# Two MLP norms moved earlier and pinned, a projection's weight split taken off GpSimd, and two roots moved, in a two-block fp32 model on one Trainium2 core

## Chip, cores and metric

The kernel runs on 1 core of one Trainium2 chip (trn2). The metric is device time in microseconds, the median of three runs. The program has 16154 instructions on five engines: TensorE (PE), VectorE (DVE), ScalarE (ACT), GpSimd (POOL) and SyncE (SP), which issues nearly all DMAs.

## What is computed

A sequence of 256 tokens with 1024 channels goes through two layers, then through a third block with other attention; all in float32. The parts that the change touches:

```python
def rmsnorm(x, g):
    y = xf * lax.rsqrt(jnp.mean(xf * xf, axis=-1, keepdims=True) + EPS)
    return (y * g.astype(jnp.float32)).astype(x.dtype)

def mixer_c(h, ...):                       # layer 1
    gate, xr = jnp.split(h @ w_in, 2, axis=-1)
    xr = causal_depthwise_conv(xr, conv_w) + conv_b
    y = rg_lru(xr, w_r, b_r, w_i, b_i, lam) * jax.nn.gelu(gate)
    return y @ w_out

def first_block(x, ...):
    for layer in range(DEPTH):             # DEPTH = 2
        h = rmsnorm(x, mix_norm[layer])
        y = mixer_ab(h, ...) if layer % 2 == 0 else mixer_c(h, ...)
        x = x + y
        x = x + sq_relu_mlp(rmsnorm(x, mlp_norm[layer]), w_up[layer], w_down[layer])
    return rmsnorm(x, final_norm)
```

`sq_relu_mlp` is `square(relu(h @ w_up)) @ w_down` with 4096 hidden channels. The second block ends with a projection, a gated residual and one more RMS norm.

## The kernel before

Activations lie with channels on the 128 partitions and the 256 tokens along the free axis. All weights, 242 units of 128 x 1024 floats (512 KB), are read from HBM once, in the order of their use. `fetch` puts a unit into one of 4 `raw` buffers by a DMA on SP's queue; `prep` (L321 to L326) splits it into a rounded part `wh` (a copy, on ACT at L323 or on DVE at L325) and the rest `wl = raw - wh` (L326, on DVE or POOL). The table `POLICY` (from L43) says which engine does which part of which unit: "ag" is ACT and POOL, "av" ACT and DVE, "vv" DVE twice. Split units stand in rings named `wh`/`wl` and `wxh`/`wxl`.

Each product is three matmuls of 128 x 256, high by high (L383), low by high (L384) and high by low (L385); a unit used for a product of 8 x 128 rows is 24 matmuls. `gpair` makes a block pair of 512 columns from two units; `krow` adds one row block `k` of a projection into four accumulators.

`mlp` (from L967) runs `p` from 0 to 15. Step `p` makes a pair of hidden blocks, `up(p)`: 48 matmuls on PE, a ReLU on ACT (`mr`, L987), the rounded square on ACT (`mah`, L988), the exact square on POOL (`ma`, L989), their difference on DVE (`mal`, L435). From `p` = 2 on it adds rows `k` = 2p-4 and 2p-3 of the down projection: 24 matmuls each. The norm of `x` is not applied to the inputs of `up` but at the end, as a factor 1/(mean square + eps), since the squared ReLU is homogeneous. That factor needs: squares on ACT and their sums on POOL (`ssq`, L437), a sum over channels on PE (`csum`, 128 x 1 matmuls, L452), mean and eps on DVE (`meaneps`, L458), a reciprocal on DVE (L1009), and `spread` (L473): `across` on PE puts the value on all partitions (128 x 128 matmuls with the identity, L470), ACT copies it (`R2`, L476). R2 is used by the projection's last rows, far behind. Layer 0's MLP also works off a list of background steps on DVE (`mod_setup`, `softplus`: rows `mdump` L915 and `sm`), one at each unit.

`layer1` (from L1027) is written in the order that PE and ACT keep (`inorder`). Its end is the projection `wo1` (`wrow(0)` to `wrow(4)`, then a tail): `root` makes the recurrence (L1106 and the scans L1108), `done(p)` multiplies with the gate (L1119) and splits the result for PE (`xr` by ACT, `ysl` by DVE L435); `more(n)` fetches and splits `n` more units.

Except where such pins stand, a scheduler in the compiler sets the order on each engine from dependencies and its own estimates, and the engines then run that order strictly, each waiting on semaphores.

`b2_kv`, `b2_attn` and `b2_out` make the second block. `b2_out` has the spread of the residual's scale (`R1`, the root of the first block's final norm) at its step p = 1, and at the end the last norm: column sums `stat` on PE (L1580), mean and eps on DVE (L458), the power -0.5 on POOL (`rsq`, L463), `across` on PE, and the multiplications of `xo` on DVE (L1614) ahead of the output DMAs.

Of the kernel before, what the change touches and what calls it, by code (L numbers as in the profile page):

```python
# [11 lines left out]
F32 = mybir.dt.float32  # L12
F32R = mybir.dt.float32r
AF = mybir.ActivationFunctionType
ALU = mybir.AluOpType
# [3 lines left out]
D = 1024  # L19
NK = 8  # L20
FF = 4096
EPS = 1e-6
# [21 lines left out]
POLICY = {n: ("ag",) for n in ("gate", "val", "q", "k", "v", "wo0")}  # L44
POLICY.update(val=("av", "ag", "av", "ag"), gate=("av", "av", "av", "ag"), xr=("av",), ri=("av",), cg=("av", "av", "av", "av", "ag", "ag", "ag", "ag"))
POLICY["wo0"] = ("ag",) * 7 + ("av",)
POLICY["up"] = ("ag",) * 4 + ("av",) * 60
POLICY["wo1"] = ("ag",) * 4 + ("av",) * 4
PADC = 30

COLS = {}
# [198 lines left out]
class Kern:  # L250
# [181 lines left out]
        self.nc.vector.scalar_tensor_tensor(l, xs, g, h.bitcast(F32), op0=ALU.mult, op1=ALU.subtract)  # L432

    def lo(self, l, src, h):
        self.nc.vector.tensor_tensor(l, src, h.bitcast(F32), op=ALU.subtract)  # L435

    def ssq(self, pool, x3):  # L437
        nc = self.nc
# [111 lines left out]
    def layer0(self, lp):  # L550
# [271 lines left out]
        for j in range(4):  # L822
            V.tensor_tensor(conv[:, j], conv[:, j], M, op=ALU.subtract)
        R2 = self.across(r2)
        yp(8, self.lasts)
# [22 lines left out]

    def proj_tail(self, acc, name, ins, gname, g0, xs, R2=None, mp=None, sums=(), after=None):

# [120 lines left out]
    def mlp(self, mp, l):  # L971
        nc = self.nc
        V, S, G, PE = nc.vector, nc.scalar, nc.gpsimd, nc.tensor
        x, xs = self.x, self.xs
        acc = [self.ps("acc") for _ in range(4)]
        A = {}
        R2 = None

        first = self.gfirst("up", xs)

        def up(p):
            ps = first[p] if p < 2 else self.gpair(("up", "up"), xs)
            r = self.t(mp, [128, 512], "mr", bufs=2)
            a = self.t(mp, [128, 512], "ma", bufs=2)
            ah = self.t(mp, [128, 512], "mah", F32R, bufs=4)
            al = self.t(mp, [128, 512], "mal", F32R, bufs=4)
            S.activation(r, ps, AF.Relu)  # L987
            S.activation(ah, r, AF.Square)  # L988
            G.tensor_tensor(a, r, r, op=ALU.mult)  # L989
            self.lo(al, a, ah)  # L990
            A[2 * p] = (ah[:, :T], al[:, :T])
            A[2 * p + 1] = (ah[:, T:], al[:, T:])

        for p in range(16):
            if l == 0 and p >= 9:
                if p == 9:
                    self.pad(self.cp, 96)
                    self.hs = [self.t(self.cp, [128, 2112], f"hc{c}", F32R) for c in "hl"]
                    self.pad(self.cp, 160)
                self.ahead = min(2 * p - 14, 13)  # L1000
            if l == 1 and p == 4:
                self.wx, self.slot = None, 0
            up(p)
            if p == 4:
                parts = self.ssq(mp, x)
            if p == 6:
                v = self.meaneps(self.csum(parts), D)
                rv = self.t(self.cp, [128, 2], "rv")
                V.reciprocal(rv, v)  # L1009
            if p == 8:  # L1010
                R2 = self.spread(mp, rv, "R2")
            if p >= 2:
                for k in (2 * p - 4, 2 * p - 3):
                    self.krow(acc, self.unit("down"), A.pop(k), k == 0, False)
        for k in range(28, 32 - NT):
            self.krow(acc, self.unit("down"), A.pop(k), False, False)
        last = l == 1
        xs = None if last else self.new_h()
        sums = [(self.s1, None), (self.s2, "fin")] if last else [(self.s1, None)]
        self.proj_tail(acc, "down", [A[k] for k in range(32 - NT, 32)], "mix", 8, xs, R2, mp, sums)  # L1020
        self.xs = xs

    def layer1(self, lp):
        nc = self.nc
        V, S, G, PE = nc.vector, nc.scalar, nc.gpsimd, nc.tensor
        x, xs = self.x, self.xs
# [9 lines left out]
        parts = [self.s1[:, 0], self.s1[:, 1]]  # L1036
# [80 lines left out]
        def done(p):  # L1117
            hp = slice(2 * p, 2 * p + 2)
            V.tensor_tensor(th[:, hp], th[:, hp], gl[:, hp], op=ALU.mult)  # L1119
            self.split(th[:, hp], ys[0][:, hp], ys[1][:, hp])  # L1120
# [4 lines left out]
        with self.inorder(*PIN):  # L1125
            conv(0, pss[0])
            conv(1, pss[1])
            self.more(3)
            self.hs, self.slot = None, self.slot % (RING + EXTRA)
            p2 = self.gpair(("xr", "xr"), xs)  # L1130
            heads(0)
            heads(1)
            gates(0, ri(0))
            conv(2, p2)
            tanhs(0)
            p3 = self.gpair(("xr", "xr"), xs)
            conv(3, p3)
            decay(0)
            decay(1)
            self.more(1)  # L1140
            cg(0)
            heads(2)
            heads(3)
            gates(1, ri(1))
            self.more(1)
            root(0)
            cg(1)
            ys = (self.t(lp, [128, 8, T], "xr", F32R), ysl)
            gelu(0)
            gelu(1)  # L1150
            done(0)
            self.more(1)
            tanhs(1)
            cg(2)
            done(1)
            decay(2)
            decay(3)
            self.more(1)
            cg(3)
            root(1)  # L1160
            gelu(2)
            gelu(3)
            self.more(2)
            acc = [self.ps("acc") for _ in range(4)]
            for k in range(4):
                if k == 2:
                    done(2)
                if k == 3:
                    done(3)
                wrow(k)  # L1170
                self.more(1 if k == 0 else 2)
            wrow(4)
        self.ahead = 2
        xs = self.new_h()
# [90 lines left out]
    def b2_kv(self, bp, ep, d):  # L1265
        nc = self.nc
        V, S, G, PE = nc.vector, nc.scalar, nc.gpsimd, nc.tensor
# [40 lines left out]
        for i in range(4):  # L1308
            w = self.unit("vb")
            for tt in range(4):  # L1310
                src = (xs, hc)[tt // 2]
                for kk in range(2):
                    k = 2 * i + kk
# [16 lines left out]
        for tt in range(4):  # L1330
            ps = self.ps()
# [5 lines left out]
        def zpair(nm, p, pool, between=None):  # L1337
            zpost(nm, p, pool, self.gp2([self.unit(nm), self.unit(nm)], xs, between))
# [8 lines left out]
        ps = self.gpair(("cq", "cq"), xs)  # L1347
# [9 lines left out]
        def cqn():  # L1357
            RQ = self.across(rq)
            for k in range(2):
                V.scalar_tensor_tensor(cf[:, k], cf[:, k], self.p("gcq", k), RQ, op0=ALU.mult, op1=ALU.mult)  # L1360
                self.split(cf[:, k], cq[0][:, k], cq[1][:, k])
        zpair("za", 1, ep, cqn)
        d.update(kb=kb, vb=vb, krh=krh, krl=krl, ck=ck, wk=wk, va=va, bp=bp)
        q8 = self.t(self.cp, [128, 2112], "hch")[:, :2048].rearrange("p (a b) -> p a b", a=8)
        for i in range(2):
            w = self.unit("uq")
            for j in range(2):
                ps = self.ps()
# [5 lines left out]
    def b2_attn(self, bp, ap, d):  # L1374
        nc = self.nc
        V, S, G, PE = nc.vector, nc.scalar, nc.gpsimd, nc.tensor
# [90 lines left out]
        tg = d["tg"] = {}  # L1467
# [24 lines left out]
        def gdone(nm, p):  # L1492
            def f(ps):
                tg[nm, p] = self.t(bp, [128, 512], f"t{nm}", bufs=2)
                S.activation(tg[nm, p], ps, AF.Tanh, scale=0.5)
            return f

        def gpair(nm, p):
# [23 lines left out]
        for i in range(n + 3):  # L1522
            if i < n:
                tag, h, qt = steps[i]
# [17 lines left out]
    def b2_out(self, op, d):  # L1542
        nc = self.nc
        V, S, G, PE = nc.vector, nc.scalar, nc.gpsimd, nc.tensor
        xs, tg = d["xs"], d["tg"]
        x = self.t(op, [128, 8, T], "xo")
# [5 lines left out]
        def yrow(k):  # L1552
            return ys[0][:, k], ys[1][:, k]
        for p in range(4):
            if p > 1:
                d["gpair"]("ga", p)
                d["gpair"]("gb", p)
                d["oproj"]("oa", p)
            d["oproj"]("ob", p)
            y = tg["ga", p]  # L1560
            V.tensor_tensor(y, y, tg["gb", p], op=ALU.add)
            self.split(self.pair(y), ys[0][:, 2 * p:2 * p + 2], ys[1][:, 2 * p:2 * p + 2])
            if p == 1:
                R1 = self.spread(op, d["r1"], "R1")
                for k in range(8):
                    V.scalar_tensor_tensor(x[:, k], x[:, k], self.p("fin", k), R1, op0=ALU.mult, op1=ALU.mult)
        def orow(w, k, ms, end):
            for m in ms:
                o = last[:, :T] if m == 7 else acc[m // 2][:, (m % 2) * T:(m % 2 + 1) * T]
                c = slice(m * 128, m * 128 + 128)  # L1570
                self.mm3(o, (w[0][:, c], w[1][:, c]), yrow(k), k == 0 and (m % 2 == 0 or m == 7), end)
        for k in range(6):
            orow(self.unit("wo2"), k, range(8), False)
        ws = [self.unit("wo2") for _ in range(2)]
        st = self.ps()
# [5 lines left out]
                          stop=end, skip_group_check=True)  # L1581
        def scale(b):
            for k in (2 * b, 2 * b + 1):
                S.activation(x[:, k], x[:, k], AF.Copy, scale=self.p("fg2", k))

        def fold(b):
            (G if b < 2 else V).tensor_tensor(sq[b][:, 0], sq[b][:, 0], sq[b][:, 1], op=ALU.add)
# [13 lines left out]
        with self.tc.issue_after(xi.ins):  # L1601
            fold(2)
        with self.tc.issue_after(si.ins):
            for b in range(1, 4):
                scale(b)
        stat(sq[0][:, 0], True)
        stat(sq[1][:, 0])
        stat(sq[3][:, 0])
        stat(sq[2][:, 0])
        stat(sq[3][:, 1], end=True)  # L1610
        RF = self.across(self.rsq(self.meaneps(st[:, :2], D)))
        for i, (k0, k1) in enumerate(((0, 1), (1, 3), (3, 5), (5, 7), (7, 8))):
            xb = x[:, k0:k1]
            V.tensor_tensor(xb, xb, self.b2(RF, k1 - k0), op=ALU.mult)  # L1614
# [22 lines left out]
```

## Time and profile before

| | us |
|---|---|
| median of 3 runs | 822.05 |
| lowest and highest run | 821.96, 824.75 |
| the profiled execution | 821.14 |
| its span | 819.4 |
| PE busy in the span | 787.9 (96%) |
| DVE, ACT, POOL busy | 576.4, 473.2, 199.0 |
| granted PE clock, mean | 0.991 |

The profiled execution is 0.91 us under the median of the runs. The span is what the trace covers; 1.7 us of the execution lie around it. A row of a timeline gives the start, the duration, the engine, the source line and the operation, and in brackets how long the engine had been idle before and what ended it. Matmuls overlap: one lasts 0.28 us by its record, and the next starts about 0.115 us after it, so the distance of starts is the price of one more matmul.

### The profile page before, as it was taken

The page shows a single profiled execution, that of the slowest core. Times are in us where ns is not written, and L with a number is a line of the kernel's source. Part 1 is how long each engine was busy: PE and PEld are TensorE (multiplying, and loading weights), DVE is VectorE, ACT ScalarE, POOL GpSimd, SP SyncE. Part 2 cuts the span into 40 slices and gives each one's busy share as a digit, 9 for nine tenths or more (in the row PEclk, how much of TensorE's full clock was granted, in tenths as well). Part 3 has the DMA queues.
Part 4 walks back from the last instruction along what each step waited for, and adds up shares of the span by engine and source line. Part 5 has one row for each costly group of instructions (what it writes and reads, how often), then busy time and mean ns, then how long its engine had stood idle before and what let it go on. Part 6 is the DMA issues. An engine that isn't in the chain of part 4 may idle for free.

```text
span 819.4 us, 16154 instructions
## 1 busy us (share of the span) xinstructions
PE 787.9 (96%) x6480; PEld 756.0 (92%) x6480; DVE 576.4 (70%) x952; ACT 473.2 (58%) x739; POOL 199.0 (24%) x151
## 2 busy tenths in 40 slices
PE   6999989999999999979999999999999999999996
PEld 5997889999999999978999999999989988889996
DVE  6999669999989787578746545557634877565843
ACT  5568656455545657877745444445626587765533
POOL 4796643011101202330531110111000022320001
PEclk9999999999999999999999999999999999999997
DMA  7874357787988832238726656664335533555531
GB/s 239 292 222 130 103 181 247 292 311 272 322 307 283 286 113 88 62 124 302 239 99 210 193 189 190 197 196 164 94 119 151 159 105 102 176 163 176 185 101 52
DMA packets 41259, 152.32 MB, mean 186 GB/s; under 512 B 4576, under 2 KB 5088, under 8 KB 39008
## 3 DMA queue, kind: packets, MB, share of 16 engines
q1 hardware_dynamic: 40752, 149.19, 55.5%
q10 hardware_dynamic: 432, 2.10, 0.7%
q8 instruction: 51, 0.84, 0.4%
q14 instruction: 24, 0.20, 0.1%
HBM read 149.17 MB, written 2.10 MB: 185 GB/s over the span
## 4 chain that ended last, share of the span: by engine, by line
PE 59%; issue 19%; DVE 8%; ACT 8%; POOL 4%; DMA 2%; SPq 0%; POOLq 0%; DVEq 0%; ACTq 0%
PE mm L383 10%; PE mm L384 10%; PE mm L385 10%; PE acc L384 7%; PE acc L383 7%; PE acc L385 7%; POOL ma L989 3%; PE acc L1423 2%; PE acc L1451 2%; PE mm L1460 2%; ACT wh L323 1%; DMA raw<-in_wst 1%; DVE wl L326 1%; PE mm L470 1%; DMA x<-in_xT 1%
## 5 line engine op out<-in xcount | busy, mean ns | idle before, releaser
L323 ACT ACTIVATE wh<-raw 128x1024 fp32r<-128x1024 f32 (+1 forms) x190 | 198.3, 1048 | 162.5 <-PE mm L384 64.2
L326 DVE TENSOR_TENSOR wl<-raw,wh 128x1024 fp32r<-128x1024 f32 (+1 forms) x159 | 197.6, 1250 | 100.1 <-ACT wh L323 98.3
L383 PE MATMUL mm<-xsh,wh 128*128 128x256 f32 x752 | 210.4, 280 | 0.0
L384 PE MATMUL mm<-xsl,wh 128*128 128x256 f32 x752 | 209.1, 278 | 0.0
L385 PE MATMUL mm<-xsh,wl 128*128 128x256 f32 x752 | 209.1, 278 | 0.0
L383 PEld LDWEIGHTS mm<-xsh,wh 128*128 128x128 f32 x752 | 141.7, 188 | 3.7 <-issue 3.3
L384 PEld LDWEIGHTS mm<-xsl,wh 128*128 128x128 f32 x752 | 141.7, 188 | 0.6 <-DVE xsl L878 0.2
L385 PEld LDWEIGHTS mm<-xsh,wl 128*128 128x128 f32 x752 | 141.3, 188 | 0.0
L989 POOL TENSOR_TENSOR ma<-mr 128x512 f32<-128x512 f32 x32 | 49.5, 1548 | 246.2 <-ACT mr L987 246.2
L384 PE MATMUL acc<-mal,wh 128*128 128x256 f32 x360 | 100.1, 278 | 1.0 <-DVE mal L435 1.0
L383 PE MATMUL acc<-mah,wh 128*128 128x256 f32 x360 | 100.3, 279 | 0.0
L385 PE MATMUL acc<-mah,wl 128*128 128x256 f32 x360 | 100.0, 278 | 0.0
L326 POOL TENSOR_TENSOR wl<-raw,wh 128x1024 fp32r<-128x1024 f32 x31 | 74.2, 2414 | 43.8 <-ACT wh L323 43.8
L323 ACT ACTIVATE wxh<-raw 128x1024 fp32r<-128x1024 f32 x47 | 49.2, 1055 | 38.8 <-DMA raw<-in_wst 34.9
L384 PEld LDWEIGHTS acc<-mal,wh 128*128 128x128 f32 x360 | 67.9, 189 | 1.2 <-DVE mal L435 1.2
L383 PEld LDWEIGHTS acc<-mah,wh 128*128 128x128 f32 x360 | 67.7, 188 | 0.0
L385 PEld LDWEIGHTS acc<-mah,wl 128*128 128x128 f32 x360 | 67.6, 188 | 0.0
L326 DVE TENSOR_TENSOR wxl<-raw,wxh 128x1024 fp32r<-128x1024 f32 x44 | 56.6, 1299 | 8.0 <-ACT wxh L323 8.0
L384 PE MATMUL mm<-xsl,wxh 128*128 128x256 f32 x208 | 58.1, 279 | 0.6 <-DVE xsl L878 0.6
L383 PE MATMUL mm<-xsh,wxh 128*128 128x256 f32 x208 | 58.3, 280 | 0.0
L385 PE MATMUL mm<-xsh,wxl 128*128 128x256 f32 x208 | 58.0, 279 | 0.0
L915 DVE CUSTOM_DVE_ANT_0 mdump<-mw,cv 128x1024 f32<-128x1024 f32 x40 | 48.7, 1217 | 2.7 <-DMA mw<-in_modw 2.6
(386 smaller groups left out, 1855.9 us busy)
## 6 DMA issues: line engine op xcount, KB each, us to landing
raw<-in_wst SPq DMA_DIRECT2D x240, 512.0 KB, 4.1
mw<-in_modw SPq DMA_DIRECT2D x12, 1024.0 KB, 7.2
nb<-in_nab SPq DMA_DIRECT2D x16, 256.0 KB, 3.7
ab<-in_alibi ACTq DMA_DIRECT2D x1, 1536.0 KB, 8.9
x<-in_xT SPq DMA_DIRECT2D x4, 256.0 KB, 4.9
cv<-in_cvec SPq DMA_DIRECT2D x1, 1024.0 KB, 4.7
cx<-in_cT SPq DMA_DIRECT2D x1, 1024.0 KB, 7.3
xd<-x SPq DMA_DIRECT2D x1, 1024.0 KB, 4.6
```

Of the source, the lines that this page charges most:

```text
L323: nc.scalar.activation(wh, r, AF.Copy)
L326: (nc.vector if lo == "v" else nc.gpsimd).tensor_tensor(wl, r, wh.bitcast(F32), op=ALU.subtract)
L383: mm(out, w[0], x[0], start=start, stop=False, skip_group_check=True)
L384: mm(out, w[0], x[1], start=False, stop=False, skip_group_check=True)
L385: return mm(out, w[1], x[0], start=False, stop=stop, skip_group_check=True)
L470: self.lasts = self.nc.tensor.matmul(ps[:, j * 128:(j + 1) * 128], rc[:, j:j + 1].to_broadcast([128, 128]), self.ident, start=True, stop=True)
L915: V.tensor_tensor_reduce(d, w, cv[:, s * 1024:(s + 1) * 1024], 0.5, 0.0, op0=ALU.mult, op1=ALU.add, accum_out=self.mod[:, s * 24 + i:s * 2 ...
L989: G.tensor_tensor(a, r, r, op=ALU.mult)
L1423: PE.matmul(sc[i], Q[tag, h][a][:, qs], K[tag, h][b], start=a + b == 0, stop=a == 1)
L1451: PE.transpose(pt[:, i * 128:(i + 1) * 128], P[:, i * 128:(i + 1) * 128], self.ident)
L1460: PE.matmul(o[64 * hh:64 * hh + 64, :T], vt[:, i, h * 64:h * 64 + 64], PTs[tag, h][:, i], start=i == 0, stop=i == 3, skip_group_check=True)
```

## The change

Four parts. (A) In both MLPs the norm's steps come earlier in the written program: squares and sums at p = 1 (before: 4), `csum`, mean and reciprocal at p = 3 (before: 6), `spread` between rows k = 2 and k = 3 of the down projection in p = 3 (before: p = 8), and PE's instructions of the whole step p = 3 are pinned to the written order. (B) In layer 1's projection the first four units, split before by ACT and POOL, are split by DVE alone (three) and by ACT and DVE (one); `done(2)` and `done(3)` come after `wrow(0)` and `wrow(1)`, and the next units are split behind their last subtraction. (C) The spread of R1 goes from `b2_out` to the end of `b2_kv`. (D) The last norm: ACT takes the square root straight from PSUM, with scale 1/D and eps as bias, DVE its reciprocal, in place of DVE's mean and POOL's power; the table for the root is loaded by a small ACT instruction behind the last tanh; two scalings of x are issued behind the root on ACT.

```diff
-POLICY["wo1"] = ("ag",) * 4 + ("av",) * 4
+POLICY["wo1"] = ("vv",) * 3 + ("av",) * 5
...
-            up(p)
-            if p == 4:
-                parts = self.ssq(mp, x)
-            if p == 6:
-                v = self.meaneps(self.csum(parts), D)
-                rv = self.t(self.cp, [128, 2], "rv")
-                V.reciprocal(rv, v)
-            if p == 8:
-                R2 = self.spread(mp, rv, "R2")
-            if p >= 2:
-                for k in (2 * p - 4, 2 * p - 3):
+            with self.inorder(PE.engine) if p == 3 else nullcontext():
+                up(p)
+                if p == 1:
+                    parts = self.ssq(mp, x)
+                if p == 3:
+                    v = self.meaneps(self.csum(parts), D)
+                    rv = self.t(self.cp, [128, 2], "rv")
+                    V.reciprocal(rv, v)
+                for k in (2 * p - 4, 2 * p - 3) if p >= 2 else ():
+                    if k == 3:
+                        R2 = self.spread(mp, rv, "R2")
                     self.krow(acc, self.unit("down"), A.pop(k), k == 0, False)
...
-            for k in range(4):
-                if k == 2:
-                    done(2)
-                if k == 3:
-                    done(3)
+            wrow(0)
+            done(2)
+            with self.tc.issue_after(self.lastlo.ins):
+                self.more(1)
+            wrow(1)
+            done(3)
+            with self.tc.issue_after(self.lastlo.ins):
+                self.more(2)
+            for k in (2, 3):
                 wrow(k)
-                self.more(1 if k == 0 else 2)
+                self.more(2)
             wrow(4)
...
         zpair("za", 1, ep, cqn)
+        d["R1"] = self.spread(bp, d["r1"], "R1")
...
             if p == 1:
-                R1 = self.spread(op, d["r1"], "R1")
                 for k in range(8):
-                    V.scalar_tensor_tensor(x[:, k], x[:, k], self.p("fin", k), R1, op0=ALU.mult, op1=ALU.mult)
+                    V.scalar_tensor_tensor(x[:, k], x[:, k], self.p("fin", k), d["R1"], op0=ALU.mult, op1=ALU.mult)
...
+        eps = self.t(op, [128, 1], "eps")
+        G.memset(eps, EPS)
+        with self.tc.issue_after(self.lastt.ins):
+            S.activation(self.warm, self.warm, AF.Sqrt)
...
         with self.tc.issue_after(si.ins):
-            for b in range(1, 4):
-                scale(b)
+            sc = scale(1)
...
-        RF = self.across(self.rsq(self.meaneps(st[:, :2], D)))
+        sd = self.t(op, [128, 2], "sd")
+        with self.tc.issue_after(sc.ins):
+            sd_ = S.activation(sd, st[:, :2], AF.Sqrt, scale=1.0 / D, bias=eps)
+        with self.tc.issue_after(sd_.ins):
+            scale(2)
+            scale(3)
+        V.reciprocal(sd, sd)
+        RF = self.across(sd)
```

How the order moves. PE, layer 0's MLP, step p = 3 of the change: the end of `up(3)` with the norm's sum, and the end of row k = 2 with the spread.

```order
L385 MATMUL mm_1720<-xsh_1312,wxl_1693 128x256
L452 MATMUL mm_1789<-ones_83,ssum_1579 128x1 x2
L383 MATMUL acc_1443<-mah_1573,wxh_1723 128x256
...
L385 MATMUL acc_1446<-mah_1573,wxl_1724 128x256
L470 MATMUL mm_1827<-ident_78,rv_1794 128x128 x2
L383 MATMUL acc_1443<-mah_1573,wxh_1753 128x256
```

Between the sum and the spread stand the 24 matmuls of row k = 2 and nothing else; before, neither stood here, and the sum came three steps later, the spread five.

DVE at the same place, before (names: `wl` a weight's low part, `sm` and `mdump` background steps, `mal` the hidden block's low part, here that of `up(3)`):

```order
L941 TENSOR_SCALAR sm_1846<-sm_1846 128x8
L326 TENSOR_TENSOR wl_1955<-raw_1952,wh_1954 128x1024
L943 TENSOR_TENSOR sm_1846<-sm_1846 128x8
L915 ISA mdump_2097,mod_1442<-mw_2055,cv_1439 128x1024
L915 ISA mod_1442 128x1
L435 TENSOR_TENSOR mal_1772<-ma_1770,mah_1771 128x512
L944 TENSOR_SCALAR sm_1846<-sm_1846 128x8
```

and in the change:

```order
L941 TENSOR_SCALAR sm_1870<-sm_1870 128x8
L326 TENSOR_TENSOR wl_1967<-raw_1964,wh_1966 128x1024
L458 TENSOR_SCALAR var_1792<-mm_1789 128x2
L943 TENSOR_TENSOR sm_1870<-sm_1870 128x8
L915 ISA mdump_2109,mod_1442<-mw_2067,cv_1439 128x1024
L915 ISA mod_1442 128x1
L435 TENSOR_TENSOR mal_1784<-ma_1782,mah_1783 128x512
L1010 RECIPROCAL rv_1794<-var_1792 128x2
L944 TENSOR_SCALAR sm_1870<-sm_1870 128x8
```

The same steps in the same order, with the mean (`var`) set behind a weight's subtraction and the reciprocal (`rv`) behind `mal`.

DVE in layer 1, ahead of the projection, in the change (`th`, `ig`, `r` are the recurrence, `ysl` a low part for PE):

```order
L1087 SCALAR_TENSOR_TENSOR ig_3753<-ig_3753,acc_4098 128x256
L325 CAST wh_4373<-raw_4371 128x1024
L326 TENSOR_TENSOR wl_4301<-raw_4298,wh_4300 128x1024
L326 TENSOR_TENSOR wl_4374<-raw_4371,wh_4373 128x1024
L1106 TENSOR_TENSOR ig_3753<-ig_3753,th_3752 128x512 x2
...
L1119 TENSOR_TENSOR th_3752<-th_3752,gl_3754 128x512
L325 CAST wh_4438<-raw_4436 128x1024
L1119 TENSOR_TENSOR th_3752<-th_3752,gl_3754 128x512
L435 TENSOR_TENSOR ysl_3747<-th_3752,xr_4292 128x512
L326 TENSOR_TENSOR wl_4439<-raw_4436,wh_4438 128x1024
```

Three casts (one stands above these rows) and three subtractions now stand among DVE's steps of the first two `done`; before, POOL had the subtractions and ACT the copies.

## Rows read from the trace of the kernel before

**Rows 1.** Page, part 1: busy us of each engine, share, instructions

```profile
PE 787.9 (96%) x6480; PEld 756.0 (92%) x6480; DVE 576.4 (70%) x952; ACT 473.2 (58%) x739; POOL 199.0 (24%) x151
```

**Rows 2.** Timeline of PE, layer 0's MLP: start us, us, operation

```profile
141.96 0.28 PE L383 MATMUL acc<-mah,wxh 128*128 128x256 f32 x1
...
147.62 0.28 PE L383 MATMUL mm<-xsh,wxh 128*128 128x256 f32 x1
```

**Rows 3.** Timelines of ACT and POOL at that place

```profile
148.02 1.06 ACT L323 ACTIVATE wh<-raw 128x1024 fp32r<-128x1024 f32 x1 [2.74 <-DMA raw<-in_wst]
...
149.65 1.54 POOL L989 TENSOR_TENSOR ma<-mr 128x512 f32<-128x512 f32 x1 [12.90 <-ACT mr L987]
```

**Rows 4.** Timeline of DVE at that place

```profile
151.12 1.21 DVE L326 TENSOR_TENSOR wl<-raw,wh 128x1024 fp32r<-128x1024 f32 x1
...
153.48 0.68 DVE L435 TENSOR_TENSOR mal<-ma,mah 128x512 fp32r<-128x512 f32 x1
```

**Rows 5.** Timelines of PE and DVE, old places of the norm's sum and reciprocal

```profile
175.88 0.50 PE L452 MATMUL mm<-ones,ssum 128*128 128x1 f32 x4
...
190.63 0.15 DVE L1009 RECIPROCAL rv<-var 128x2 f32<-128x2 f32 x1
```

**Rows 6.** Timeline of PE, old spread, first and last matmul behind it

```profile
198.94 0.61 PE L470 MATMUL mm<-ident,rv 128*128 128x128 f32 x4
...
199.51 0.28 PE L384 MATMUL acc<-mal,wh 128*128 128x256 f32 x1
...
282.36 0.28 PE L383 MATMUL acc<-mah,wxh 128*128 128x256 f32 x1
```

**Rows 7.** Timelines of PE and DVE, layer 1's MLP

```profile
409.25 0.28 PE L383 MATMUL acc<-mah,wxh 128*128 128x256 f32 x1
...
406.69 4.92 DVE L326 TENSOR_TENSOR wl<-raw,wh 128x1024 fp32r<-128x1024 f32 x4
```

**Rows 8.** Waits of PE, 348.4 to 384: us in total, times, longest

```profile
PE acc L385 <- POOL wl L326: 2.9, 2, 1.5
PE acc L384 <- DVE ysl L435: 2.5, 2, 1.6
```

**Rows 9.** Stretches of PE: us, busy, granted clock, DMA share, GB/s

```profile
348.40:356.00 7.60, 5.46 (x37) 0.85 0.14 44
```

**Rows 10.** Timeline of PE in layer 1's projection

```profile
354.64 0.42 PE L383 MATMUL acc<-xr,wh 128*128 128x256 f32 x1
...
357.19 0.28 PE L383 MATMUL acc<-xr,wh 128*128 128x256 f32 x1
```

**Rows 11.** Timelines of POOL and DVE, layer 1's projection

```profile
357.62 5.19 POOL L326 TENSOR_TENSOR wl<-raw,wh 128x1024 fp32r<-128x1024 f32 x2 [3.42 <-ACT wh L323]
...
341.25 1.47 DVE L1119 TENSOR_TENSOR th<-th,gl 128x512 f32<-128x512 f32 x2
...
357.73 5.63 DVE L1119 TENSOR_TENSOR th<-th,gl 128x512 f32<-128x512 f32 x2
```

**Rows 12.** Line 1326 on DVE: ns min/median/max, first and last start

```profile
L1326 DVE CAST wkh<-wh x1: 421/421/421, 594.8 to 594.8; 128x512 fp32r<-128x512 f32 x1
```

**Rows 13.** Timeline of PE ahead of the old spread of R1

```profile
750.01 0.28 PE L385 MATMUL mm<-ob,wl 128*128 128x256 f32 x1
...
753.78 0.28 PE L385 MATMUL mm<-ob,wl 128*128 128x256 f32 x1
753.89 0.61 PE L470 MATMUL mm<-ident,r 128*128 128x128 f32 x4
```

**Rows 14.** Timelines of DVE, POOL, PE, the last norm

```profile
811.08 0.16 DVE L458 TENSOR_SCALAR var<-mm 128x2 f32<-128x2 f32 x1 [1.31 <-PE mm L1580]
811.32 0.71 POOL L463 TENSOR_TENSOR rc<-var,mhalf 128x2 f32<-128x2 f32 x1 [2.69 <-DVE var L458]
...
812.08 1.22 PE L470 MATMUL mm<-ident,rc 128*128 128x128 f32 x4 [1.04 <-POOL rc L463]
```

**Rows 15.** Timeline of ACT, a small operation

```profile
137.94 0.21 ACT L936 ACTIVATE sm<-sm 128x8 f32<-128x8 f32 x1
```

More of the change, by code (lines that the diff above doesn't have):

```diff
@@ L434, in lo @@
     def lo(self, l, src, h):
-        self.nc.vector.tensor_tensor(l, src, h.bitcast(F32), op=ALU.subtract)
+        self.lastlo = self.nc.vector.tensor_tensor(l, src, h.bitcast(F32), op=ALU.subtract)
     def ssq(self, pool, x3):
@@ L1494, in f @@
                 tg[nm, p] = self.t(bp, [128, 512], f"t{nm}", bufs=2)
-                S.activation(tg[nm, p], ps, AF.Tanh, scale=0.5)
+                self.lastt = S.activation(tg[nm, p], ps, AF.Tanh, scale=0.5)
             return f
@@ L1583, in scale @@
             for k in (2 * b, 2 * b + 1):
-                S.activation(x[:, k], x[:, k], AF.Copy, scale=self.p("fg2", k))
+                i = S.activation(x[:, k], x[:, k], AF.Copy, scale=self.p("fg2", k))
+            return i
         def fold(b):
```

## Prediction

> **What bounds the kernel now.** The page's first part comes first: PE is busy for 787.9 of 819.4 us [rows 1]. The reader should see that only two things can change the time much: a stretch in which PE stands still, and the distance at which its matmuls follow each other. So the timeline of PE comes next, then, at each place where the change gives PE something new to wait for, the timelines of the engines that must deliver it; the order listings say what stands ahead of what there, the trace says when.
>
> The distance between matmuls is not one number. From 141.96 to 147.62 there are 48 matmuls, 117.9 ns each [rows 2]. Behind the old spread of layer 0's MLP, 731 recorded matmuls start from 199.51 to 282.36, 113.5 ns each [rows 6]. The slower pace lasted until the very spread at 198.94. In the same way the 33 starts from 750.01 to 753.78 are 117.8 ns apart, up to the spread of R1 at 753.89 [rows 13], and behind that the pace is again the quicker one until the last sums. So a spread seems to set the quick pace, and a sum by 128 x 1 matmuls the slow one. I take 4.4 ns a matmul for this.
>
> **A, layer 0's MLP.** Nothing is added or removed; steps are moved. On PE the sum now stands ahead of row k = 2, which began at 141.96 [rows 2], and the spread behind that row. The sum's group lasted 0.50 us by its record [rows 5]; I put 0.4 for it, and the row's 24 matmuls take 24 x 0.118 = 2.8. PE is at the spread at 141.96 + 0.4 + 2.8 = 145.2.
>
> What must be ready there is the reciprocal, and DVE runs its own strict order. In the changed order the mean stands behind a weight's subtraction and the reciprocal behind `mal` of `up(3)`. Before, that subtraction ran at 151.12 and that `mal` from 153.48 to 154.16 [rows 4]. They weren't late by chance: the weight's copy on ACT started at 148.02 after 2.74 us of waiting for its DMA, and POOL's square, from which `mal` is made, started at 149.65 [rows 3]. All of this lies upstream of the moved steps, and the listing shows these steps in the same order as before. With the mean's 0.16 and the reciprocal's 0.15 (same operations, [rows 5, 14]) in between, the reciprocal ends at about 154.4. PE is pinned, so it has nothing to do in place of the spread: it **stands from 145.2 to 154.4, 9.2 us**. That DVE lags like this shows in the old place too: the sum was on PE at 175.88 and its reciprocal on DVE at 190.63, 14.8 us later [rows 5], and nobody noticed, since the spread came only at 198.94 [rows 6]. The bounds are nothing (DVE has caught up) and 9.5 (DVE at its time, plus two handoffs); I take 9.2.
>
> The wait also costs clock. In layer 1's projection, where PE waited less at a time, the granted clock fell to 0.85 over a stretch [rows 9], and 12 matmuls from 354.64 to 357.19 took 212 ns each [rows 10], which is the 1.2 GHz level: 12 x (212 - 118) = 1.1 us. After a longer wait it can hardly be less; bounds 0 and 2.3, I take **1.4**.
>
> In return the quick pace would start behind the new spread and not at 198.94. Between 145.2 and 198.94 lie some 450 matmuls (53.7 / 0.118, less the sum): 450 x 4.4 ns = **-2.0**. If the spread doesn't set the quick pace after such a wait, this is nothing, and the slow pace may go on to 282.36: 730 x 4.4 ns = +3.2.
>
> **A, layer 1's MLP.** The same move. PE would be at the spread at 409.25 + 0.4 + 2.8 = 412.5; DVE's four subtractions end at 406.69 + 4.92 = 411.6 [rows 7], and with mean and reciprocal behind them the value is there at 411.9: in time by 0.6. But if part B brings PE here 4.4 us earlier and DVE doesn't come as much earlier, up to 3.8 of it is lost again; bounds 0 and 3.8. The subtractions write into buffers that PE frees, so most of them move along: I take **+1.0**. The quick pace comes earlier by the distance from the old sum to the old spread, as long as in layer 0 (198.94 - 175.88, 192 matmuls): **-0.8**.
>
> **B, layer 1's projection.** Removed: four subtractions on POOL, 2.6 us each in the pair at 357.62 [rows 11], and three copies on ACT of about 1.06 [rows 3]. Added on DVE: three casts and four subtractions. A subtraction has 1.23 in the group of four [rows 7]; a cast of 512 columns took 0.42 [rows 12], so a cast of 1024 takes between 0.42 and 0.84, and I take 0.7. Together 3 x 0.7 + 4 x 1.23 = 7.0 us of DVE's time. PE waited 2.9 us for POOL's subtractions in this stretch and 2.5 for `ysl` [rows 8]. The first goes, and with it the clock's 1.1 (1.2 with the first matmul). The second hangs on DVE's gate products: two took 5.63 beside POOL's subtractions and 1.47 without them [rows 11], so 4.2 go. But ahead of them DVE now has a cast and a subtraction more (1.9), and its first recurrence starts later by some 2, since two casts and two subtractions stand ahead of it: 0.3 is left of the 4.2. Sum: 2.9 + 1.2 + 0.3 = **-4.4**. Bounds: 0, if the new DVE work delays the recurrence by as much as is won, and -6.6, if PE's waits (2.9 + 2.5) and the clock's 1.2 all go. SP's order is the same here; weights are fetched as their buffers come free, so a few transfers start earlier.
>
> **C, R1's spread.** PE does the same four matmuls at another place, under other PE work, and ACT its copy: nothing. But the old spread turned the slow pace to the quick one at 753.89 [rows 13]. The last sums begin some 480 matmuls later; if nothing else turns it, they go at the slow pace: 480 x 4.4 ns = **+2.1**. Bounds 0 and 2.1, and up to 1 more where the spread now stands; the trace has no spread without this turn in such a place, so I take 2.1.
>
> **D, the last norm.** From DVE's mean at 811.08 to PE's start at 812.08 it was 1.00 us: 0.16, POOL's 0.71 and handoffs of 0.13 [rows 14]. Now ACT's root, some 0.21 as the small ACT operation [rows 15], the reciprocal's 0.15 [rows 5] and as much for handoffs: 0.5. **-0.5**; bounds 0 (ACT still at a scaling) and -0.65. Two scalings move behind the root; the multiplications they serve wait for the spread anyway. The table for the root is loaded behind the last tanh, well ahead of the end.
>
> **Sum.** 9.2 + 1.4 - 2.0 + 1.0 - 0.8 - 4.4 + 2.1 - 0.5 = +6.0. The profiled execution took 821.14, so 827.1; the median of the runs lies 0.9 above it: **828.0**.
>
> The Trainium skill, page "TensorE: Matmul & The Clock Gate", section "Wait — 56ns, not 53.3ns?", gives a warm matmul one fixed distance: columns at 2.4 GHz plus about 2.5 ns, by my estimate 109 ns for 256 columns. The trace disagrees twice, with 113.5 and 117.9 and a switch between them. By the page's one pace the terms -2.0, -0.8 and +2.1 would be nothing, and the sum 828.7.
>
> **The rivals.**
> 1. *The reciprocal is in time, and the change is faster.* It decides at one point: reciprocal done by 145.2. Then the 9.2 and the 1.4 fall away, and the 1.0, if it holds in layer 1 too: 822.05 - 2.0 - 0.8 - 4.4 + 2.1 - 0.5 = 816.4. For it: the sum of squares is done early, and DVE's mean and reciprocal are 0.3 us of work. Against it: DVE's order puts both behind work that waits for a DMA, 9 us too late. Chance 0.12.
> 2. *The wait comes as forecast, but the pace stays slow behind it* until 282.36: 828.0 + 2.0 + 3.2 = 833.2. For it: every sum in the trace leaves the slow pace, and the spreads that turned it had no wait. Chance 0.25.
> 3. *Part B doesn't do what it says*: DVE's new 7 us delay the recurrence as much as POOL's exclusion did. 828.0 + 4.4 - 1.0 = 831.4. Chance 0.12.
> 4. *B gains its upper bound and C costs nothing*: 828.0 - 2.2 - 2.1 = 823.7. Chance 0.10.
>
> The forecast itself has 0.41, with 826 to 830 for its own sizes. About 0.5% (4.1 us) is what a measurement of this kernel can tell from no change, so the bounds are 817.9 and 826.2. Faster: rival 1 and a little, 0.13. Same: rival 4 and the forecast's low end, 0.12. Slower: 0.75. The range leaves out rival 1 and the ends: 823.0 to 834.0.
>
> **What would show it.** In the changed profile: a wait of PE ahead of the spread (line 470) in layer 0's MLP of about 9 us, released by DVE's reciprocal; a dip of the granted clock behind it, then starts 113.5 ns apart. In layer 1's projection no wait for POOL, gate products of 0.7 us each, and the following MLP about 4 us earlier relative to the MLP before. Behind 754, starts 118 ns apart. A PE that passes line 470 without a wait would make the prediction wrong.

## The result

| | before | changed |
|---|---|---|
| median of 14 runs | 823.61 | 828.89 |
| lowest and highest | 821.15, 825.96 | 824.24, 836.20 |
| profiled execution, its span | 821.14, 819.4 | 832.15, 830.4 |

The ratio is 1.0075 with a 95% interval of [1.0046, 1.0104], 6.2 us (3.8 to 8.6) slower; the forecast was 828.0, which is 6.0 over the median known then, and "slower". An execution of the kernel e9 below at a granted clock of 0.75 took 983.5 us; such executions are left out of the ratios, and no row of e9 is read. The two profiled executions are 11.0 us apart, more than the medians, and the pages of one execution explain that one alone. That executions differ by themselves is seen before the change has any effect: the same matmuls between 20 and 40 us are 117.8 ns apart in the trace of before and 113.4 in the trace after. There it is the changed kernel that is quicker, so this isn't what sets the two apart.

The waits of PE in the changed kernel, whole span (us in total, times, longest):

```profile
PE mm L470 <- DVE sm L944: 9.3, 1, 9.3
...
PE acc L384 <- DVE ysl L435: 2.6, 2, 1.5
PE mm L470 <- DVE rv L1010: 2.1, 1, 2.1
```

The first line is new, and as long as the forecast said. Its place on PE, then ACT, POOL and DVE around it (timeline; answers [rows 2 to 4]):

```profile
142.91 0.28 PE L452 MATMUL mm<-ones,ssum 128*128 128x1 f32 x2
...
155.68 1.19 PE L470 MATMUL mm<-ident,rv 128*128 128x128 f32 x4 [9.34 <-DVE sm L944]
156.52 0.56 PE L383 MATMUL acc<-mah,wxh 128*128 128x256 f32 x1
...
161.18 0.28 PE L383 MATMUL mm<-xsh,wxh 128*128 128x256 f32 x1
...
149.19 1.06 ACT L323 ACTIVATE wh<-raw 128x1024 fp32r<-128x1024 f32 x1 [2.67 <-DMA raw<-in_wst]
150.81 1.60 POOL L989 TENSOR_TENSOR ma<-mr 128x512 f32<-128x512 f32 x1 [12.73 <-ACT mr L987]
146.55 1.23 DVE L326 TENSOR_TENSOR wl<-raw,wh 128x1024 fp32r<-128x1024 f32 x1 [2.00 <-ACT wh L323]
...
147.81 1.17 DVE L915 CUSTOM_DVE_ANT_0 mdump<-mw,cv 128x1024 f32<-128x1024 f32 x1
...
150.29 1.22 DVE L915 CUSTOM_DVE_ANT_0 mdump<-mw,cv 128x1024 f32<-128x1024 f32 x1
...
152.35 1.21 DVE L326 TENSOR_TENSOR wl<-raw,wh 128x1024 fp32r<-128x1024 f32 x1
153.49 0.15 DVE L458 TENSOR_SCALAR var<-mm 128x2 f32<-128x2 f32 x1
...
154.78 0.68 DVE L435 TENSOR_TENSOR mal<-ma,mah 128x512 fp32r<-128x512 f32 x1
155.38 0.15 DVE L1010 RECIPROCAL rv<-var 128x2 f32<-128x2 f32 x1
```

PE has the sum at 142.91 and is ready for the spread at 146.3. ACT's copy waits 2.67 us for its DMA and ends at 150.25; DVE's subtraction comes at 152.35, the mean behind it, `mal` at 154.78, and only then the reciprocal, in time for a spread at 155.68. From 146.55 on DVE has no idle time: its subtraction isn't waiting for the copy any more, it stands behind three background steps (`mdump`) and small ones, and a fourth `mdump` stands between the mean and `mal`. The view names `sm` as the releaser, the small operation next to the reciprocal. Behind it the row's 24 matmuls take from 156.52 to 161.18, 4.66 us and not 2.83: the granted clock is down (stretches of PE: us, busy, granted clock, DMA share, GB/s; answers [rows 9]).

```profile
148.00:156.00 8.00, 0.32 (x1) 0.64 0.61 204
156.00:162.00 6.00, 6.00 (x35) 0.63 1.00 384
162.00:170.00 8.00, 8.00 (x70) 1.00 0.97 365
```

Where the time of this pair went, by the starts of the same steps in both traces: layer 0's MLP (from its first matmul to the next layer's) 180.2 before, 194.0 after, **+13.8**; layer 1 up to its projection 55.5 and 56.7; the projection 31.6 and 24.8, **-6.7**; layer 1's MLP 180.9 and 182.6, **+1.7**; from the second block's first matmul to the last of 128 x 256 247.7 and 247.7; the tail -0.3; ahead of all this +1.3 that no edit touches.

In the projection the waits are gone or other ones (waits of PE, 364.8 to 389.7; answers [rows 8]):

```profile
PE acc L383 <- DVE th L1099: 1.2, 2, 0.7
PE acc L385 <- DVE wl L326: 1.0, 1, 1.0
```

and DVE's gate products are short again, beside casts of 0.69 us (timeline of DVE; answers [rows 11, 12]):

```profile
359.16 0.68 DVE L1119 TENSOR_TENSOR th<-th,gl 128x512 f32<-128x512 f32 x1
359.76 0.69 DVE L325 CAST wh<-raw 128x1024 fp32r<-128x1024 f32 x1
373.72 1.27 DVE L1119 TENSOR_TENSOR th<-th,gl 128x512 f32<-128x512 f32 x2
```

The last norm, ACT's root, DVE's reciprocal and the spread (timeline; answers [rows 14]):

```profile
822.47 0.26 ACT L1621 ACTIVATE sd<-mm,eps 128x2 f32<-128x2 f32 x1 [0.45 <-PE mm L1588]
822.76 0.17 DVE L1625 RECIPROCAL sd<-sd 128x2 f32<-128x2 f32 x1 [1.66 <-ACT sd L1621]
823.08 1.19 PE L470 MATMUL mm<-ident,sd 128*128 128x128 f32 x4 [0.70 <-DVE sd L1625]
```

From the first of the last column sums (L1588 at 820.09, before L1580 at 808.76) to the spread it is 2.99 us, before 3.32.

### The profile page after: what moved, and what is told of

Read it like the earlier page. It is cut to its first block, busy times and chain, and to the rows that moved or that the text cites. A ratio compares the mean times of both kernels' runs of the same rounds, so it can differ in the third digit from the quotient of the medians.

```text
span 830.4 us, 16149 instructions
## 1 busy us (share of the span) xinstructions
PE 790.9 (95%) x6480; PEld 759.6 (91%) x6480; DVE 582.5 (70%) x959; ACT 473.3 (57%) x739; POOL 191.4 (23%) x147
## 4 chain that ended last, share of the span: by engine, by line
PE 68%; DVE 11%; ACT 8%; DMA 6%; issue 3%; POOL 2%; SPq 0%; DVEq 0%; ACTq 0%; POOLq 0%
PE mm L383 11%; PE mm L384 11%; PE mm L385 11%; PE acc L383 9%; PE acc L384 9%; PE acc L385 9%; DMA raw<-in_wst 5%; PE acc L1428 2%; DVE wl L326 2%; ACT wh L323 2%; PE acc L1456 2%; PE mm L1465 2%; DVE mm L612 1%; DVE wxl L326 1%; PE mm L470 1%
## 5 line engine op out<-in xcount | busy, mean ns | idle before, releaser
L323 ACT ACTIVATE wh<-raw 128x1024 fp32r<-128x1024 f32 (+1 forms) x187 | 195.3, 1048 | 162.5 <-PE mm L384 66.2
L326 DVE TENSOR_TENSOR wl<-raw,wh 128x1024 fp32r<-128x1024 f32 (+1 forms) x163 | 205.4, 1266 | 109.6 <-ACT wh L323 107.6
L326 POOL TENSOR_TENSOR wl<-raw,wh 128x1024 fp32r<-128x1024 f32 x27 | 65.3, 2440 | 29.7 <-ACT wh L323 29.7
L326 DVE TENSOR_TENSOR wxl<-raw,wxh 128x1024 fp32r<-128x1024 f32 x44 | 54.4, 1250 | 8.6 <-ACT wxh L323 8.4
L915 DVE CUSTOM_DVE_ANT_0 mdump<-mw,cv 128x1024 f32<-128x1024 f32 x40 | 51.1, 1277 | 3.7 <-DMA mw<-in_modw 3.4
```

The lines of the kernel that those rows point to most:

```text
L323: nc.scalar.activation(wh, r, AF.Copy)
L326: (nc.vector if lo == "v" else nc.gpsimd).tensor_tensor(wl, r, wh.bitcast(F32), op=ALU.subtract)
L915: V.tensor_tensor_reduce(d, w, cv[:, s * 1024:(s + 1) * 1024], 0.5, 0.0, op0=ALU.mult, op1=ALU.add, accum_out=self.mod[:, s * 24 + i:s * 2 ...
```

## The experiments

Theory: DVE's strict order and late inputs make the pinned spread of layer 0's MLP wait, which costs about 10 us; B and D gain some 4 to 5; the rest is small. All ratios are to the kernel before, run on the same chip.

**e1: layer 0's old places.** In `mlp` of the changed kernel (also the form of the next edits):

```diff
-            with self.inorder(PE.engine) if p == 3 else nullcontext():
+            NS, NC, NK_, PINS = ((4, 6, 12, ()), (1, 3, 3, (3,)))[l]
+            with self.inorder(PE.engine) if p in PINS else nullcontext():
...
```

(`NS`, `NC` and `NK_` then stand where the steps of the squares, of the sum and the row of the spread stood as numbers.)

> The changed kernel with layer 0's norm steps back at their old places (p = 4, 6, 8, unpinned); all else as changed. Theory (DVE is 9 us late for the pinned spread): PE's wait of 9.3 us at line 470 in layer 0's MLP and the clock's dip behind it are gone, so the time falls by 10 to 12 us against the changed kernel and lies 3 to 6 us below the kernel before. Rival (PE's idle time is only brought forward, or the loss is the slow pace of 117.8 ns): the time falls by 0 to 3 us at most.

Measured 819.75, ratio 0.9954 [0.9932, 0.9975]: 3.8 us under the kernel before, 10.0 under the changed one (1.0075 - 0.9954). No wait is left at line 470 in layer 0's MLP, and layer 1's has 0.2. The theory holds, at the low end of its 10 to 12 us; the loss is this one move.

**e2: only that move, in the kernel before** (`((1, 3, 3, (3,)), (4, 6, 12, ()))[l]`).

> The kernel before with only layer 0's norm steps moved and pinned as in the change. Theory: one wait of 9 to 10 us at the spread, 1.5 to 2 us of low clock behind it; in sum 9 to 13 us slower than the kernel before, by the pace that PE has behind it. Rival (later stages absorb it): less than 4 us slower.

Measured 835.66, ratio 1.0130 [1.0102, 1.0158], 10.7 us slower. Nothing absorbs the wait, which is 7.7 us here, less than the 9 to 10 expected (timeline of PE):

```profile
156.59 0.76 PE L470 MATMUL mm<-ident,rv 128*128 128x128 f32 x2 [7.70 <-DVE sm L944]
```

The rest is the clock behind it and the pace: some 1390 of this MLP's matmuls go at the slow distance, against 575 in the trace of before.

**e3: only part B.** The `POLICY` line and the block with `done(2)`, `done(3)` of the change in the kernel before.

> The kernel before with only layer 1's projection changed (weights split by DVE, other order). Theory: no wait for POOL in the projection, which gets 4 to 7 us shorter; the norm of layer 1's MLP is at its old place, so nothing is given back there: 4 to 7 us faster than the kernel before. Rival (DVE's 7 us of new work delay the recurrence as much): within 1.5 us of the kernel before.

Measured 820.60, ratio 0.9965 [0.9939, 0.9992]: 2.9 us faster (0.7 to 5.0). In its trace the projection takes 26.5 us, 5.0 less than before, without a wait for POOL. The direction is the theory's, the size is below its 4 to 7; the interval reaches into them, and into the rival's 1.5 too. That the wait for POOL goes is shown by the trace, but a gain of 4 us isn't shown by the times.

**e4: the spread two rows later in both MLPs**, ahead of k = 5 (`(1, 3, 5, (3, 4))` for both).

> The changed kernel with the spread two rows later in both MLPs (ahead of row k = 5, in p = 4, which is pinned too); the sums stay at p = 3. PE then reaches the spread some 11 us after the sum. Theory: DVE's value is there by then, so both waits at line 470 (9.3 and 2.1 us) fall under 0.5 us, and the time is 11 to 14 us below the changed kernel, 5 to 8 below the kernel before. Rival (pinning or the sum's early place is what costs): the time stays within 3 us of the changed kernel.

Measured 826.23, ratio 1.0028 [1.0000, 1.0056]. Missed: both waits at line 470 are gone, but the gain against the changed kernel is 3.9, not 11 to 14, and nearer to the rival's 3. Waits of PE, whole span:

```profile
PE acc L384 <- DVE mal L435: 3.6, 4, 1.3
...
PE mm L452 <- POOL ssum L445: 2.5, 1, 2.5
```

New waits for `mal` stand late in layer 0's MLP (1.3, 1.1 and 0.7 us, at 285.82, 244.72 and 232.06), one for the context's sum of squares in layer 1's, and in this execution that MLP ran at 117.8 ns from 430 on, some 1100 matmuls of 4.4 ns more each. That these make up the rest is read from one execution, and what the pins by themselves cost wasn't run.

**e8: DVE's reciprocal first**, with PE's order as changed.

```diff
-                    V.reciprocal(rv, v)
+                    ri_ = V.reciprocal(rv, v)
+                    if l == 0:
+                        hold.enter_context(self.tc.issue_after(ri_.ins))
```

(`hold` is closed at p = 9.)

> The changed kernel, and in layer 0's MLP all of DVE's instructions that are written behind the reciprocal (the next weights' subtractions, the background steps) are queued behind it, up to p = 8; PE's order is as changed. Theory (the reciprocal stands too far back in DVE's strict order): DVE has the value at about 143, PE passes line 470 with a wait under 0.5 us, and the time is 9 to 12 us below the changed kernel. Rival (DVE or its inputs are late there whatever the order): a wait of over 3 us remains at line 470, or its size comes back as waits for weights in the next steps.

Measured 829.72, ratio 1.0066 [1.0042, 1.0090]: not faster than the changed kernel. The first half of the theory holds, PE passes the spread without a wait; the second falls, since the time comes back (timeline of DVE and PE, then the waits of PE):

```profile
144.03 0.16 DVE L458 TENSOR_SCALAR var<-mm 128x2 f32<-128x2 f32 x1 [5.07 <-PE mm L452]
144.22 0.17 DVE L1013 RECIPROCAL rv<-var 128x2 f32<-128x2 f32 x1
...
146.76 0.61 PE L470 MATMUL mm<-ident,rv 128*128 128x128 f32 x4
...
PE acc L384 <- DVE mal L435: 5.0, 4, 2.7
...
PE acc L383 <- ACT mah L989: 3.5, 2, 3.4
```

DVE stood still for 5 us to have the reciprocal early. At the end of this MLP PE waited for `mal` and `mah` and the clock fell. Stretches of DVE here (us, busy, granted clock, DMA share, GB/s):

```profile
110.00:150.00 40.00, 24.67 (x29) 0.99 0.57 189
280.00:300.00 20.00, 14.62 (x20) 0.66 0.73 235
```

and in the kernel before:

```profile
110.00:150.00 40.00, 32.74 (x40) 1.00 0.74 249
150.00:200.00 50.00, 49.69 (x78) 1.00 0.79 287
```

DVE was full in the kernel before, 49.7 of 50 us from 150 to 200, and up to 150 it did 8.1 us less in e8 (24.67 against 32.74). What it loses ahead of that is missing behind it: PE's 96% hides that this MLP has two bounds. The edit holds back every later step of DVE, the weights' subtractions too. A reciprocal that only passes the background steps wasn't run.

**e5: part C undone**, on e1: R1's spread back in `b2_out`.

> The kernel of the run with layer 0's old norm places (e1), with R1's spread also back in the output stage (part C undone). Theory of the prediction (the old spread turned the slow pace of matmuls to the quick one): undoing C gives 2.1 us back, the last 480 matmuls run 113.5 ns apart. Rival, from the traces so far (a spread without a wait swaps the two paces, whichever was there): the pace ahead of the old spread is the quick one in some executions, and then the spread makes it slow to the end; on the mean C is worth between 0 and 2 us of gain.

Measured 819.46, ratio 0.9960 [0.9936, 0.9984], e1 has 0.9954: C is worth nothing that these runs can tell. In e5's trace the spread at 750.79 found the quick pace and left the slow one up to the end, as in e2 and e3; in the kernel before it was the other way round [rows 13], as in e10. In all six traces with C (changed, e1, e4, e6, e7, e8) the last 480 matmuls ran at the quick one.

**e6 and e7: one and two spreads more** in layer 1's MLP, on e1, results unused (e7 has `range(2)`); PE's step p = 6, in which they stand, is pinned:

```diff
+                    if l == 1 and k == 9:
+                        for _ in range(1):
+                            self.across(rv)
```

> The kernel of e1 with one more spread whose result nobody uses, pinned ahead of row k = 9 in layer 1's MLP, where the pace had been 113.4 ns. Theory (a spread without a wait swaps the pace): from there to the end of this MLP, some 950 matmuls, the starts are 117.8 ns apart, 4.2 us longer, with 0.4 for the spread: 4 to 5 us slower than e1. Rival (a spread always leaves the quick pace): 113.4 ns stays, 0.4 us slower than e1.

> The same with two spreads one behind the other at that place. Theory (each swaps the pace): back at 113.4 ns behind the second, 0.8 us slower than e1. Rival (a spread leaves the slow pace where it found the quick one, for another reason than a swap): 117.8 ns, 5 us slower than e1.

Measured 823.18 and 823.61, ratios 1.0001 [0.9977, 1.0024] and 1.0007 [0.9978, 1.0037]: 3.9 and 4.4 us slower than e1. Timeline of PE around the one spread:

```profile
445.71 0.28 PE L383 MATMUL acc<-mah,wh 128*128 128x256 f32 x1
...
447.41 0.60 PE L470 MATMUL mm<-ident,rv 128*128 128x128 f32 x4
...
447.98 0.28 PE L384 MATMUL acc<-mal,wh 128*128 128x256 f32 x1
...
449.39 0.28 PE L384 MATMUL acc<-mal,wh 128*128 128x256 f32 x1
```

From 445.71 to 447.41 there are 15 matmuls, 113 ns each; from 447.98 to 449.39 twelve, 117.5, and so on to the end of the MLP, without a wait at the spread. One unused spread of 0.4 us costs 4. Two of them (0.8) leave the slow pace too, so a simple swap by each falls, as does "a spread makes it quick".

**e10: layer 1's norm alone**, in the kernel before (`((4, 6, 12, ()), (1, 3, 3, (3,)))[l]`).

> The kernel before with only layer 1's norm steps moved and pinned. Theory of the prediction: without part B the reciprocal is there 0.6 us ahead of PE, so no wait at line 470 in this MLP over 0.3 us, and within 2 us of the kernel before. Rival (the wait of 2 us seen in the changed kernel belongs to the move itself, not to PE's earlier arrival): a wait of 1.5 us or more stands there too.

Measured 824.17, ratio 1.0009 [0.9979, 1.0040], a wait of 0.8 us at the spread. This lies between the theory's 0.3 and the rival's 1.5: the reciprocal is late without B too. With B the traces of the changed kernel, e1, e5, e6, e7 and e8 show 2.1, 0.2, 1.5, 3.1, 1.9 and nothing, so that B makes the wait longer isn't shown.

**e9: part A undone in both MLPs**, B, C and D kept (`(4, 6, 12, ())` for both).

> The changed kernel with part A undone in both MLPs (B, C and D stay). Theory: no wait at line 470 in either MLP, so B's and D's gains stand alone: 3 to 6 us below the kernel before, and as fast as e1 or up to 2 us faster, since e1 still waited 0.2 to 3 us at the spread of layer 1's MLP. Rival (the earlier norm helps layer 1's MLP by its pace): 1 to 2 us slower than e1.

Measured 818.15, ratio 0.9939 [0.9916, 0.9962], 5.0 us under the kernel before: the fastest kernel here, though not told apart from e1 (0.9954).

## Why the prediction was right

- **Layer 0's wait**: 9.2 forecast, 9.3 measured. DVE's order was as read and the reciprocal done at 155.5 (154.4 was worked out, and the whole stage came 1.3 later). But the prediction's reason, inputs that come late, is only half right: at that point DVE wasn't waiting for the copy or for POOL's square in either trace. In before it ran from 145.32 to 154.24 without idle time, in the changed kernel from 146.55 to 155.53, and part of what stood ahead were its own background steps. Without them the next bound would be POOL's square, done at 152.41; with `mal` and the reciprocal behind it the value would be there at about 153.2, and the wait 7 us: an estimate from these rows, no run tests it. The move alone is worth 10.7 us (e2) and its removal 10.0 (e1), against 8.6 as the sum of its three terms.
- **The clock**: 1.4 forecast, 4.66 - 2.83 = 1.8 measured, and 0.5 more for the spread itself. The granted clock fell to 0.64 and 0.63 over the two stretches.
- **The pace behind the spread**: wrong. -2.0 was forecast because unstalled spreads had turned the slow pace to the quick one. Behind the waits of 9.3 (changed) and 7.7 us (e2) it stayed at 117.8 ns, until the next spread at 316. Of the pair's +13.8 some 3.1 are left for it: 13.8 less the wait of 9.3, the clock's 1.8 and 0.5 for the slower spread, and then 0.9 more, by which the waits for `mal` got shorter (1.9 to 1.0). It fits the count: 1280 matmuls of this MLP go at the slow distance, 705 more than before, at 4.4 ns each. That is the second rival's mechanism, on top of the forecast's. And no sum had set the slow pace of [rows 2]: it began at 130.67, behind a wait of 1.0 us for `mal`.
- **Layer 1's MLP**: +1.0 for the wait; 2.1 in the changed kernel. The step "in time by 0.6" was wrong by 1.4 there, since a wait of 0.8 stands without B too (e10). The -0.8 for its pace: behind the first sum 216 matmuls went at the slow distance before and 96 in the changed kernel, -0.5.
- **B**: -4.4 forecast; -2.9 (0.7 to 5.0) alone, -6.7 and -5.0 in the projection of two traces. Right in sign, and POOL's 2.9 went as forecast. But all 2.5 of the wait for `ysl` went too, where the forecast counted 0.3, and 1.0 for a weight's low part from DVE is new.
- **C**: +2.1 forecast, nothing measured. The step that failed is the reading that the old spread made the end quick: it left it quick in two traces (before, e10) and slow in three (e2, e3, e5). As all six with C end quick, C may even gain up to 2.1 us; e1 and e5 can't tell.
- **D**: -0.5 forecast, -0.33 measured (2.99 and 3.32), in the pair.

So the wait and the clock carried the forecast, and that the total came out to 0.2 us (+6.0 and +6.2) is luck, since single terms missed to both sides: layer 0's move cost some 2 us more than its three terms, B by itself gained 1.5 less, and C's 2.1 did not come. The parts as they were measured, 10.7 (e2), 0.7 (e10), -2.9 (e3) and -0.3 (D), make 8.2, inside the interval of 3.8 to 8.6. The first rival, a reciprocal in time, did not happen in the changed kernel or in e2; e8, which makes it happen by force, shows that the time forecast for it, 816.4, isn't to be had that way: 829.7.

The Trainium skill, page "TensorE: Matmul & The Clock Gate", section "Wait — 56ns, not 53.3ns?", has one fixed distance for a warm matmul. None of the eleven traces that were read agrees: all have stretches at 113.4 and at 117.8 ns at a full granted clock, and e6 moves a stretch from one to the other.

## What to carry to other kernels

Before a step is pinned earlier on the busiest engine, ask the other engines' timelines when its input is made there, in their strict order, and what stands ahead of it (here, background steps among others); a value that came 15 us late without harm becomes a wait of 9 us when its user moves. And look at how full the engine is that makes it: DVE was busy for 49.7 of 50 us behind PE's 96%, and putting the value ahead of all its later work only moved the loss. Undo a change part by part before dropping it: here three of its four parts make a kernel that is 0.6% faster.

## What was not expected

Matmuls of 128 x 256 run at one of two distances, 113.4 or 117.8 ns, at full granted clock, and keep it for hundreds of instructions. Other matmuls in between switch it: e6 shows it for one spread. In the eleven traces that were read, where both sides show a clear pace, the sums by 128 x 1 matmuls left the slow one in 69 of 74 cases; spreads without a wait changed the pace, whichever it was, in 69 of 70; spreads with a wait in 7 of 20. But a wait of PE switches it too, with no other matmul near: in e4 at 232.06, 244.72 and 285.82, behind the three waits for `mal`, it goes to 117.8, back to 113.4 and to 117.8 again. The same steps have it differently from trace to trace ahead of any edit. This may be why the changed kernel's runs lie up to 12 us apart, but it isn't shown, as there is one trace of each kernel. The cause isn't settled: two spreads in a row (e7) switched it once, not twice.
